# A hybrid diffusion step: the gate rows' chain in two parts by tokens, and the first output gate moved ahead of the gate transposes

## The chip, the cores and the metric

The kernel runs on one core of a Trainium2 chip. The metric is the device time of one execution in microseconds (us); lower is better. The engines are named as in the profile: PE is TensorE's matmul, PEld its weight load, DVE is VectorE, ACT is ScalarE, POOL is GpSimd, SP is SyncE. Each engine works through its own list of instructions; semaphores tie the lists together.

## The reference, cut to what matters

One layer takes 1024 sample (latent) tokens and 256 context tokens, 1280 in all, of width 1024. `u = RMSNorm(x)*(1+scale)+shift` goes through one wide projection. One of the three branches behind it is a bidirectional mLSTM with four heads. Its gates are 16 columns of the projection (input and forget gate, two directions, four heads). Per head and direction:

```
logf = log_sigmoid(f)
b    = cumsum(logf)                       # within a chunk
m_t  = max(b + m, max_s(b_t - b_s + i_s))   # running stabiliser
w_state = exp(bL - b + i - m_new);  decay = exp(bL + m - m_new)
h    = num / max(|den|, exp(-m_t))
y    = sigmoid(o_pre) * rmsnorm(h)
```

Sample tokens start both scans from a cached state (`m0`), context tokens from zero; no scan crosses from one kind of token to the other. `sigmoid(o_pre)` is the output gate, one projection of 128 columns a head.

## The kernel before, in words

Tokens lie in three groups (`GROUPS`): 512 and 512 sample tokens and 256 context tokens. Activations are held as pairs of fp32r tiles, a high and a low part (`uT[k][g]`, named `u0h`, `u0l`, and `u0c` for both parts of the context). A product (`dense`, lines 117 to 125) multiplies high by high, high by low and low by high, so a projection of 128 columns is 24 matmuls a group. Weights are loaded by SP, cut into `hi` on ACT and `lo` on DVE (`load_w`, lines 93 and 94).

Results go to PSUM banks. `ps_mm` is a ring of three banks for projections, `ps_sd` one of five for everything else. A fourth `ps_mm` product therefore waits until the first of the ring has been evicted, which ACT does (`evict_kqv`, line 329: `kT`, `vT`, `qT`, and `kq`, which holds k and q of the context).

In the first part of the program the engines' names stand for `Pinned` wrappers (line 43), which keep the instructions of an engine in the order in which they are written. Behind it a scheduler orders the rest, and may move what is not pinned into gaps.

The pinned loop `steps` goes over groups 1 and 2 and eight `k`. At each step it transposes a tile of x (`tr`), modulates one (`mc`: an ACT ACTIVATE into `val_u`, a DVE CAST and TENSOR_TENSOR into the pair `u..`), and adds one `k` to the first head's k and v (`p_k`, `p_v`). At step (2, 0) the gates of groups 0 and 1 are multiplied (`gates_of`, into `pg`); ACT copies them to `pgs`, and SP moves their low rows to other partitions (`pgl`). At step (2, 3) `gates_add` adds the halves on DVE into rows of `z`, 36 partitions by 1280 tokens. Behind the loop come the evictions of group 2, and the gates of group 2.

Then, unpinned, comes the chain of the gate rows: log-sigmoid (lines 419 to 428), the two kinds of scan (433 to 442), small copies of the values at chunk ends (`bL`, `mnew`, `mprev`), three exponentials (464, 468, 470), over all 1280 tokens at once. Lines 474 to 493 transpose the rows on PE (`pc`, 30 transposes) into `gcol` and spread the decays by one matmul (`pd`). The heads need `gcol` and `dmb`. While the chain runs, the scheduler fills PE with what needs only `uT`: q0 of groups 1 and 2, the first head's output gate (`p_o`), and k of the second head.

Of the kernel before, what the change touches and what calls it, by code (L numbers as in the profile page):

```python
# [7 lines left out]
F32 = mybir.dt.float32  # L8
F32R = mybir.dt.float32r
AF = mybir.ActivationFunctionType  # L10
ALU = mybir.AluOpType
# [18 lines left out]
I_XP, I_SU, I_Q, I_K, I_V, I_O, I_BR = 0, 4, 8, 12, 16, 20, 24  # L30
# [18 lines left out]
def hybrid_step(  # L49
# [7 lines left out]
    engines = nc.vector, nc.scalar, nc.gpsimd, nc.tensor  # L57
# [280 lines left out]
    nc.gpsimd.dma_start(sel, sel8)  # L338

    R36 = 36  # L340
    zr = [z[0:R36, i * T : (i + 1) * T] for i in range(7)]

    gparts = {}

# [15 lines left out]
    def gates_add(g):  # L360
        t0, n = GROUPS[g]
        both, low = (t[:, :n] for t in gparts[g])
        V.scalar_tensor_tensor(zr[0][:, t0 : t0 + n], both[0:36], bgt[:, 0:1], low[0:36], ALU.add, ALU.add)
        V.tensor_tensor(zr[1][:, t0 : t0 + n], both[64:100], low[64:100], ALU.add)


    begun = {nm: (w, []) for nm, w in (("k0", w_k0), ("v0", w_v0), ("q0", w_q0))}
# [44 lines left out]
    V, A, G, PE = engines  # L412
    gates_add(2)

    def chunks(ap):
        return ap.rearrange("p (c t) -> p c t", t=P)

    zi, zf, z2, z3, z4, z5, z6 = zr
    V.tensor_scalar(zf, zf, bgt[:, 1:2], None, ALU.add)
    A.activation(z2, zf, AF.Abs)  # L420
    A.activation(z6, z2, AF.Sigmoid)
    A.activation(z2, z2, AF.Exp, scale=-1.0)
    V.tensor_scalar(z3, z2, 1.0, None, ALU.add)
    A.activation(z4, z3, AF.Ln)
    V.scalar_tensor_tensor(z5, z3, -1.0, z2, ALU.add, ALU.subtract)
    V.tensor_tensor(z5, z5, z6, ALU.mult)
    V.tensor_tensor(z4, z4, z5, ALU.subtract)
    V.scalar_tensor_tensor(zf, zf, 0.0, z4, ALU.min, ALU.subtract)
    G.memset(z4, 1.0)
    G.memset(chunks(z4)[0:32, :, 0:1], 0.0)  # L430
    G.memset(chunks(z4)[32:36, :, 127:128], 0.0)
    rev = slice(None, None, -1)
    V.tensor_tensor_scan(z2[0:32], z4[0:32], zf[0:32], 0.0, ALU.mult, ALU.add)
    V.tensor_tensor_scan(z2[32:36, rev], z4[32:36, rev], zf[32:36, rev], 0.0, ALU.mult, ALU.add)
    for lo_, hi_, smp in ((0, NSAMP, True), (NSAMP, T, False)):
        ini = m0t if smp else None
        V.tensor_tensor_scan(
            z3[0:32, lo_:hi_], zf[0:32, lo_:hi_], zi[0:32, lo_:hi_],
            ini[0:32] if smp else 0.0, ALU.add, ALU.max)
        V.tensor_tensor_scan(  # L440
            z3[32:36, lo_:hi_][:, rev], zf[32:36, lo_:hi_][:, rev], zi[32:36, lo_:hi_][:, rev],
            ini[32:36] if smp else 0.0, ALU.add, ALU.max)
    bL = cp.tile([R36, NT], F32, name="bL")
    mnew = cp.tile([R36, NT], F32, name="mnew")
    mprev = cp.tile([R36, NT], F32, name="mprev")
    V.memset(mprev, 0.0)
    b3, m3 = chunks(z2), chunks(z3)
    V.tensor_copy(bL[0:32], b3[0:32, :, 127])
    V.tensor_copy(bL[32:36], b3[32:36, :, 0])
    V.tensor_copy(mnew[0:32], m3[0:32, :, 127])  # L450
    V.tensor_copy(mnew[32:36], m3[32:36, :, 0])
    V.tensor_copy(mprev[0:32, 0:1], m0t[0:32])
    V.tensor_copy(mprev[0:32, 1:8], mnew[0:32, 0:7])
    V.tensor_copy(mprev[0:32, 9:10], mnew[0:32, 8:9])
    V.tensor_copy(mprev[32:36, 7:8], m0t[32:36])
    V.tensor_copy(mprev[32:36, 0:7], mnew[32:36, 1:8])
    V.tensor_copy(mprev[32:36, 8:9], mnew[32:36, 9:10])
    G.dma_start(m_out[0], mnew[0:4, 9:10])
    G.dma_start(m_out[1], mnew[32:36, 8:9])
    bm = cp.tile([R36, NT], F32, name="bm")  # L460
    V.tensor_tensor(bm, bL, mnew, ALU.subtract)
    dec = cp.tile([R36, NT], F32, name="dec")
    V.tensor_tensor(dec, bm, mprev, ALU.add)
    A.activation(dec, dec, AF.Exp)

    V.tensor_tensor(zi, zi, z2, ALU.subtract)
    V.tensor_tensor(z2, z2, z3, ALU.subtract)
    A.activation(z5, z3, AF.Exp, scale=-1.0)
    V.tensor_tensor(chunks(z4), chunks(zi), bm.unsqueeze(2).to_broadcast([R36, NT, P]), ALU.add)
    A.activation(z4, z4, AF.Exp)  # L470


    gcol = cp.tile([P, 3, NT, 8], F32, name="gcol")
    for qi, src in enumerate((zi, z5, z4)):
        pc = ps_sd(f"pc{qi}")
        pcv = pc[:, 0 : NT * R36].rearrange("p (c j) -> p c j", j=R36)
        for c in range(NT):
            PE.transpose(pcv[:, c, :], src[:, c * P : (c + 1) * P], ident[0:R36, 0:R36])
        for d in range(2):
            V.tensor_copy(gcol[:, qi, :, 4 * d : 4 * d + 4], pcv[:, :, 32 * d : 32 * d + 4])  # L480
    GC, EM, EWS = (gcol[:, i] for i in range(3))

    dsel = tmp("dsel")[0:R36, 0:160].rearrange("p (q j c) -> p q j c", q=2, j=8)
    for qi, src in enumerate((dec, mprev)):
        V.tensor_tensor(
            dsel[:, qi], src.unsqueeze(1).to_broadcast([R36, 8, NT]),
            sel[0:36, :].unsqueeze(2).to_broadcast([R36, 8, NT]), ALU.mult)
    ones36 = tmp("ones36")[0:R36, 0:P]
    V.memset(ones36, 1.0)
    pd = ps_sd("pd")  # L490
    PE.matmul(pd[:, 0:160], ones36, dsel.rearrange("p q j c -> p (q j c)"), start=True, stop=True)
    dmb = cp.tile([P, 2, 8, NT], F32, name="dmb")
    V.tensor_copy(dmb.rearrange("p q j c -> p (q j c)"), pd[:, 0:160])
    decb, mpb = dmb[:, 0], dmb[:, 1]

    rhl = []
    for g in range(3):
# [38 lines left out]
    so = z[:, 7730:9010]  # L536
# [8 lines left out]

    def head_proj(h):
        tiles = {}
        kq = kq0 if h == 0 else slot(f"kq{h}", F32)
        for nm, idx in (("k", I_K), ("v", I_V), ("q", I_Q)):
            w, lst = begun.pop(f"{nm}{h}", (None, []))  # L550
            tiles[nm] = lst
            proj(idx + h, f"{nm}{h}", lambda g, ps: lst.append(evict_kqv(nm, h, g, ps, kq)), w=w, groups=range(len(lst), 3))
        return tiles["k"], tiles["v"], tiles["q"]

    def head(h, kT, vT, qT):
# [39 lines left out]
        def ev_o(g, ps):  # L595
            t0, n = GROUPS[g]
            A.activation(so[:, t0 : t0 + n], ps[:, :n], AF.Sigmoid)

        ssq = small([P, 16], f"ssq{h}")
        for g in range(3):  # L600
# [45 lines left out]
            if g == 0:  # L646
                proj(I_O + h, f"o{h}", ev_o)
            ps = ps_sd(f"th{h}_{g}")
            for cl in range(ncn):
# [886 lines left out]
```

## Time and profile before

| what | value |
|---|---|
| median of 3 runs | 1946.46 us (1945.74 to 1949.13) |
| profiled execution, its own time | 1947.31 us |
| its span, first to last instruction | 1945.5 us |
| mean granted TensorE clock | 0.994 |
| DMA | 313.32 MB, mean 161 GB/s |
| instructions on PE, DVE, ACT, POOL | 10136, 2207, 1768, 380 |

A row of the timeline gives the start, the duration, the engine, the line, the operation, and what is written from what; a bracket at its end gives the idle time of that engine just before and what ended it. L43 is the pinned helper, so pinned instructions all bear that line and are told apart by their tiles. A row of the waits gives the total, the number of times and the longest. PE's matmul ends are modelled.

### The profile page before, as it was taken

The page shows a single profiled execution, that of the slowest core. Times are in us where ns is not written, and L with a number is a line of the kernel's source. Part 1 is how long each engine was busy: PE and PEld are TensorE (multiplying, and loading weights), DVE is VectorE, ACT ScalarE, POOL GpSimd, SP SyncE. Part 2 cuts the span into 40 slices and gives each one's busy share as a digit, 9 for nine tenths or more (in the row PEclk, how much of TensorE's full clock was granted, in tenths as well). Part 3 has the DMA queues.
Part 4 walks back from the last instruction along what each step waited for, and adds up shares of the span by engine and source line. Part 5 has one row for each costly group of instructions (what it writes and reads, how often), then busy time and mean ns, then how long its engine had stood idle before and what let it go on. Part 6 is the DMA issues. An engine that isn't in the chain of part 4 may idle for free.

```text
span 1945.5 us, 28129 instructions
## 1 busy us (share of the span) xinstructions
PE 1903.0 (98%) x10136; PEld 1627.5 (84%) x10136; DVE 1294.0 (67%) x2207; ACT 861.7 (44%) x1768; POOL 378.2 (19%) x380
## 2 busy tenths in 40 slices
PE   6999999999999999999999999999999999999998
PEld 3778888998788888888888887888888888888886
DVE  6574443347759889875675599888776655744665
ACT  7444464653243333343123374555454545443443
POOL 1200001107302424220000015444431110000003
PEclk9999999999999999999999999999999999999999
DMA  9211111012635445469522435776773586654444
GB/s 361 85 59 33 43 39 40 27 56 70 203 119 165 149 158 164 153 211 321 163 97 98 152 120 212 253 264 246 259 269 136 193 333 203 210 170 151 165 133 159
DMA packets 149318, 313.32 MB, mean 161 GB/s; under 512 B 17550, under 2 KB 40818, under 8 KB 147130
## 3 DMA queue, kind: packets, MB, share of 16 engines
q1 hardware_dynamic: 107354, 220.73, 33.9%
q0 software_dynamic: 15520, 57.75, 7.8%
q10 hardware_dynamic: 26304, 33.04, 4.7%
q8 instruction: 79, 1.29, 0.3%
q14 instruction: 61, 0.50, 0.1%
HBM read 217.59 MB, written 93.36 MB: 160 GB/s over the span
## 4 chain that ended last, share of the span: by engine, by line
PE 87%; DVE 4%; DMA 3%; POOL 2%; ACT 1%; issue 1%; SPq 0%; POOLq 0%; ACTq 0%; DVEq 0%
PE w L1403 6%; PE w L1404 6%; PE w L1405 6%; PE pb L1050 3%; PE pb L1051 3%; PE pb L1052 3%; PE fT L892 3%; PE fT L890 3%; PE fT L891 3%; PE fB L891 2%; PE fB L890 2%; PE fB L892 2%; PE fT_g L892 2%; PE fT_g L890 2%; PE fT_g L891 2%; PE po L1168 2%
## 5 line engine op out<-in xcount | busy, mean ns | idle before, releaser
L1242 POOL TENSOR_TENSOR z<-z 128x512 f32<-128x512 f32 x64 | 100.1, 1564 | 123.3 <-DMA z<-in_w_ff 120.6
L947 DVE TENSOR_TENSOR z<-z 128x512 f32<-128x512 f32 x112 | 88.7, 792 | 2.5
L527 POOL PARTITION_ALL_REDUCE acc<-acc x16 | 54.6, 3446 | 184.0 <-DVE acc L521 113.6
L521 DVE SCALAR_TENSOR_TENSOR acc<-z,scond,acc 128x512 f32<-128x512 f32 x112 | 86.1, 816 | 0.0
L1357 POOL TENSOR_TENSOR rs_y<-rs_y,neghalf 128x1 f32<-128x1 f32 x10 | 9.6, 966 | 333.0 <-DVE rs_y L1356 333.0
L1208 ACT ACTIVATE z<-z 128x512 f32<-128x512 f32 x64 | 40.5, 632 | 69.8 <-DVE z L956 36.7
L972 ACT ACTIVATE z<-z 128x512 f32<-128x512 f32 x48 | 30.3, 632 | 59.1 <-DVE z L956 23.1
L130 POOL TENSOR_TENSOR rs_h<-rs_h,neghalf 128x4 f32<-128x4 f32 (+1 forms) x12 | 10.9, 910 | 200.5 <-DVE rs_h L129 200.3
L653 DVE SCALAR_TENSOR_TENSOR yc<-th,ccol,z 128x512 f32<-128x512 f32 (+1 forms) x12 | 7.9, 661 | 58.2 <-PE th L651 58.2
L1056 DVE TENSOR_TENSOR sg<-pb,sg 128x512 f32<-128x512 f32 (+1 forms) x48 | 28.7, 600 | 26.7 <-PE pb L1052 26.5
L881 ACT CAST hi_wb<-raw_wb 128x512 fp32r<-128x512 f32 x24 | 14.8, 620 | 64.4 <-PE pb L1051 37.6
L1209 ACT ACTIVATE z<-z 128x512 f32<-128x512 f32 x64 | 40.3, 629 | 1.1
L1171 DVE TENSOR_TENSOR po<-po,gt 128x512 f32<-128x512 f32 (+1 forms) x24 | 14.6, 607 | 35.1 <-PE po L1170 35.0
L1233 POOL DMA_DIRECT2D scr_s<-x x48 | 26.3, 549 | 53.1 <-DVE x L1227 47.6
L738 POOL TENSOR_TENSOR z<-z 128x1024 f32<-128x1024 f32 (+13 forms) x20 | 33.6, 1702 | 6.9 <-ACT z L722 4.6
L528 POOL TENSOR_TENSOR acc<-acc,bt 1x512 f32<-1x512 f32 x16 | 23.5, 1480 | 58.4 <-issue 58.4
L1174 ACT ACTIVATE po<-z 128x512 f32<-128x512 f32 (+1 forms) x24 | 12.7, 529 | 48.5 <-DVE z L1173 34.2
L587 DVE SCALAR_TENSOR_TENSOR z<-z,dmb,kv 128x129 f32<-128x129 f32 x56 | 16.6, 345 | 21.8 <-PE kv L576 21.3
L1057 DVE TENSOR_TENSOR z<-z,sg 128x512 f32<-128x512 f32 (+1 forms) x48 | 28.7, 601 | 1.2
L640 DVE TENSOR_TENSOR den<-den,gcol 128x2 f32<-128x2 f32 x40 | 6.2, 159 | 31.0 <-ACT den L639 29.9
L43 PE MATMUL pm<-wah,shl 128*4 128x512 f32 x32 | 13.8, 461 | 13.2 <-ACT wah L43 13.2
L130 POOL TENSOR_TENSOR rs_f<-rs_f,neghalf 128x4 f32<-128x4 f32 (+1 forms) x3 | 3.3, 1092 | 116.9 <-DVE rs_f L129 116.9
(5136 smaller groups left out, 7288.9 us busy)
## 6 DMA issues: line engine op xcount, KB each, us to landing
z<-in_w_ff SPq DMA_DIRECT2D x64, 512.0 KB, 5.5
z<-in_w_ada SPq DMA_DIRECT2D x64, 256.0 KB, 3.1
scr_t<-z POOLq DMA_DIRECT2D x16, 1024.0 KB, 4.9
z<-in_w_in SPq DMA_DIRECT2D x24, 512.0 KB, 4.3
scr_g<-z ACTq DMA_DIRECT2D x48, 256.0 KB, 2.0
sg<-scr_g SPq DMA_DIRECT2D x48, 256.0 KB, 4.5
scr_h<-z ACTq DMA_DIRECT2D x48, 256.0 KB, 3.6
scr_s<-x POOLq DMA_DIRECT2D x48, 256.0 KB, 4.3
```

The lines of the kernel that those rows point to most:

```text
L521: V.scalar_tensor_tensor(acc[j], raw, scond[:, k, j : j + 1], acc[j], ALU.mult, ALU.add)
L890: PE.matmul(ps, whi[:, s], ahi, start=first and k == ks[0], stop=False)
L891: PE.matmul(ps, whi[:, s], alo, start=False, stop=False)
L892: PE.matmul(ps, wlo[:, s], ahi, start=False, stop=end and k == ks[-1])
L947: V.tensor_tensor(out, x, y, op)
L1050: PE.matmul(pb[:, :n], whi[:, s], yh, start=kc == 0, stop=False)
L1051: PE.matmul(pb[:, :n], whi[:, s], yl, start=False, stop=False)
L1052: PE.matmul(pb[:, :n], wlo[:, s], yh, start=False, stop=kc == 3)
L1242: G.tensor_tensor(out, x, y, ALU.subtract)
L1403: PE.matmul(banks[j], h_[:, s], rh, start=fp == 0, stop=False)
L1404: PE.matmul(banks[j], l_[:, s], rh, start=False, stop=False)
L1405: PE.matmul(banks[j], h_[:, s], rl, start=False, stop=fp == NFP - 1)
```

## The change

The chain becomes a function `gate_rows(groups)`, called twice: for groups 0 and 1 (1024 sample tokens) inside the pinned loop at step (2, 6), and for group 2 (256 context tokens) behind the pinned part. The transposes become `gate_columns(groups)`, called twice as well. q0 of groups 1 and 2, the first head's output gate and k of the second head are now written out around them. DVE, ACT and POOL are unpinned behind the loop as before, while PE stays pinned until the second `gate_columns`. The gates are added at (2, 6) instead of (2, 3). The multiplication by a sigmoid in the correction of the logarithm is left out, with its row of `z`; the free room lets `so`, the output gate, lie beside the gate rows.

```diff
-        if (g, k) == (2, 3):
-            gates_add(0)
-            gates_add(1)
+        if (g, k) == (2, 6):
+            gate_rows((0, 1))
...
     gates_of(2)
-    V, A, G, PE = engines
-    gates_add(2)
+    V, A, G = engines[:3]
+
+    for g in (1, 2):
+        ps = ps_mm(f"p_q0{g}")
+        dense(ps, w_q0, uT, g)
+        begun["q0"][1].append(evict_kqv("q", 0, g, ps, kq0))
+    so = z[:, 7730:9010]
...
+    w_o0 = load_w(w_in[I_O], "o0")
+    for g in range(3):
+        ps = ps_mm(f"p_o0{g}")
+        dense(ps, w_o0, uT, g)
+        ev_o(g, ps)
+    gate_rows((2,))
+    gate_columns((0, 1))
+    kq1 = slot("kq1", F32)
+    w_k1 = load_w(w_in[I_K + 1], "k1")
+    begun["k1"] = w_k1, []
+    for g in range(3):
+        ps = ps_mm(f"p_k1{g}")
+        dense(ps, w_k1, uT, g)
+        begun["k1"][1].append(evict_kqv("k", 1, g, ps, kq1))
+    gate_columns((2,))
+    PE = engines[3]
```

The new functions, cut to their core (`y..` are the rows' columns from `lo_` to `hi_`):

```diff
+    def gate_rows(groups):
...
+        G.memset(y4, 1.0)
...
+        for g in groups:
+            gates_add(g)
+        V.tensor_scalar(yf, yf, bgt[:, 1:2], None, ALU.add)
+        A.activation(y2, yf, AF.Abs)
+        A.activation(y2, y2, AF.Exp, scale=-1.0)
+        V.tensor_scalar(y3, y2, 1.0, None, ALU.add)
+        V.scalar_tensor_tensor(y5, y3, -1.0, y2, ALU.add, ALU.subtract)
+        A.activation(y3, y3, AF.Ln)
+        V.tensor_tensor(y3, y3, y5, ALU.subtract)
+        V.scalar_tensor_tensor(yf, yf, 0.0, y3, ALU.min, ALU.subtract)
...
+        A.activation(dec[:, cc], dec[:, cc], AF.Exp)
+        A.activation(y5, y3, AF.Exp, scale=-1.0)
+        V.tensor_tensor(yi, yi, y2, ALU.subtract)
+        V.tensor_tensor(y2, y2, y3, ALU.subtract)
+        V.tensor_tensor(chunks(y4), chunks(yi), bm[:, cc].unsqueeze(2).to_broadcast([R36, nch, P]), ALU.add)
+        A.activation(y4, y4, AF.Exp)
+
+    def gate_columns(groups):
...
+        for qi, src in enumerate((yi, y5, y4)):
...
+            for c in range(nch):
+                PE.transpose(pcv[:, c, :], src[:, c * P : (c + 1) * P], ident[0:R36, 0:R36])
...
+        PE.matmul(pd[:, 0 : 16 * nch], ones36, dsel.rearrange("p q j c -> p (q j c)"), start=True, stop=True)
```

The four scans (the running maximum, then the cumulative sum, each for 32 and for 4 partitions) stand where the third mark is.

The first place is DVE's list at the end of the loop. Before, the four gate adds (`z<-pgs`) stand in front of the last three pairs `u5c` to `u7c`, and behind these come the low parts of the weights of o and k:

```order
L43 SCALAR_TENSOR_TENSOR z<-pgs_920,bgt,pgl_921 36x512
L43 TENSOR_TENSOR z<-pgs_920,pgl_921 36x512
L43 SCALAR_TENSOR_TENSOR z<-pgs_941,bgt,pgl_942 36x512
L43 TENSOR_TENSOR z<-pgs_941,pgl_942 36x512
L43 CAST u5c<-val_u_5_1000 128x256
L43 TENSOR_TENSOR u5c<-val_u_5_1000,u5c 128x256
```

On the same engine of the changed kernel the adds stand behind `u7c`, and the sample rows follow at once (`36x1024`), with the two low parts between them:

```order
L43 CAST u7c<-val_u_7_1026 128x256
L43 TENSOR_TENSOR u7c<-val_u_7_1026,u7c 128x256
L43 SCALAR_TENSOR_TENSOR z<-pgs_928,bgt,pgl_929 36x512
L43 TENSOR_TENSOR z<-pgs_928,pgl_929 36x512
L43 SCALAR_TENSOR_TENSOR z<-pgs_949,bgt,pgl_950 36x512
L43 TENSOR_TENSOR z<-pgs_949,pgl_950 36x512
L94 TENSOR_TENSOR lo_o_1164<-raw_o_1161,hi_o_1163 128x1024
L43 TENSOR_SCALAR z<-z,bgt 36x1024
L94 TENSOR_TENSOR lo_k_1323<-raw_k_1320,hi_k_1322 128x1024
L43 TENSOR_SCALAR z<-z 36x1024
```

So the pairs moved ahead of the adds, and the sample rows' chain moved ahead of everything that DVE does for the context's gates.

The second place is ACT's list behind the last modulation. Before, it cuts the weights and evicts k and v of group 2, the context's gates and q0, and then begins the rows (`z<-z`):

```order
L93 CAST hi_o_1420<-raw_o_1418 128x1024
L43 ACTIVATE kq_669<-p_k_957 128x256
L93 CAST hi_k_1673<-raw_k_1671 128x1024
L43 ACTIVATE vT_2_1046<-p_v_958 128x256
L43 COPY pgs_1065<-pg_1048 128x256
L329 ACTIVATE qT_1_1204<-p_q_1179 128x512
L329 ACTIVATE kq_669<-p_q_1206 128x256
L93 CAST hi_v_1759<-raw_v_1757 128x1024
L420 ACTIVATE z<-z 36x1280
```

In the changed kernel, in ACT's list from the second weight on:

```order
L93 CAST hi_k_1322<-raw_k_1320 128x1024
L43 ACTIVATE z<-z 36x1024
L43 ACT_TABLE_LOAD
L43 ACTIVATE z<-z 36x1024
L43 ACT_TABLE_LOAD
L43 ACTIVATE z<-z 36x1024
L43 ACT_TABLE_LOAD
L43 ACTIVATE dec<-dec 36x8
L43 ACTIVATE z<-z 36x1024 x2
L43 ACTIVATE kq_669<-p_k_965 128x256
L43 ACTIVATE vT_2_1085<-p_v_966 128x256
L43 COPY pgs_1104<-pg_1087 128x256
```

All the sample rows' ACT work now stands ahead of the three evictions.

The third place is PE's list where q0 of group 2 begins (`p_q<-u0c`). Before, the context's gates stand ahead of it, and q0 of group 1 lies further ahead, between the steps of k and v:

```order
L43 MATMUL pg_1048<-u5c,wgs_804 128x256 x2
L43 MATMUL pg_1048<-u6c,wgs_804 128x256 x2
L43 MATMUL pg_1048<-u7c,wgs_804 128x256 x2
L123 MATMUL p_q_1206<-u0c,hi_q_665 128x256
L124 MATMUL p_q_1206<-u0c,hi_q_665 128x256
L125 MATMUL p_q_1206<-u0c,lo_q_666 128x256
```

In the changed kernel PE's list has q0 of group 1 directly ahead of it:

```order
L43 MATMUL p_q_1108<-u7h_873,hi_q_665 128x512
L43 MATMUL p_q_1108<-u7l_874,hi_q_665 128x512
L43 MATMUL p_q_1108<-u7h_873,lo_q_666 128x512
L43 MATMUL p_q_1135<-u0c,hi_q_665 128x256 x2
L43 MATMUL p_q_1135<-u0c,lo_q_666 128x256
```

q0 of group 1 moved behind the context's gates; o0, the sample transposes, k of the second head and the context's transposes follow in the order of the diff.

More of the change, by code (lines that the diff above doesn't have):

```diff
@@ L340, in hybrid_step @@
     R36 = 36
-    zr = [z[0:R36, i * T : (i + 1) * T] for i in range(7)]
+    zr = [z[0:R36, i * T : (i + 1) * T] for i in range(6)]
     gparts = {}
@@ L364, in gates_add, with chunks @@
         V.tensor_tensor(zr[1][:, t0 : t0 + n], both[64:100], low[64:100], ALU.add)
+    def chunks(ap):
+        return ap.rearrange("p (c t) -> p c t", t=P)
+    zi, zf, z2, z3, z4, z5 = zr
+    rev = slice(None, None, -1)
+    bL = cp.tile([R36, NT], F32, name="bL")
+    mnew = cp.tile([R36, NT], F32, name="mnew")
+    mprev = cp.tile([R36, NT], F32, name="mprev")
+    bm = cp.tile([R36, NT], F32, name="bm")
+    dec = cp.tile([R36, NT], F32, name="dec")
+    gcol = cp.tile([P, 3, NT, 8], F32, name="gcol")
@@ new lines, in hybrid_step @@
+    GC, EM, EWS = (gcol[:, i] for i in range(3))
+    dmb = cp.tile([P, 2, 8, NT], F32, name="dmb")
+    decb, mpb = dmb[:, 0], dmb[:, 1]
+    V.memset(mprev, 0.0)
+    def gate_rows(groups):
+        lo_, hi_ = GROUPS[groups[0]][0], sum(GROUPS[groups[-1]])
+        smp = lo_ == 0
+        c0, c1 = lo_ // P, hi_ // P
+        nch = c1 - c0
+        yi, yf, y2, y3, y4, y5 = (t[:, lo_:hi_] for t in zr)
+        cc = slice(c0, c1)
+        G.memset(y4, 1.0)
+        G.memset(chunks(y4)[0:32, :, 0:1], 0.0)
+        G.memset(chunks(y4)[32:36, :, 127:128], 0.0)
+        for g in groups:
[8 more added lines that the diff above has]
+        V.scalar_tensor_tensor(yf, yf, 0.0, y3, ALU.min, ALU.subtract)
+        for r, d in ((slice(0, 32), slice(None)), (slice(32, 36), rev)):
+            V.tensor_tensor_scan(
+                y3[r][:, d], yf[r][:, d], yi[r][:, d], m0t[r] if smp else 0.0, ALU.add, ALU.max)
+        for r, d in ((slice(0, 32), slice(None)), (slice(32, 36), rev)):
+            V.tensor_tensor_scan(y2[r][:, d], y4[r][:, d], yf[r][:, d], 0.0, ALU.mult, ALU.add)
+        b3, m3 = chunks(y2), chunks(y3)
+        V.tensor_copy(bL[0:32, cc], b3[0:32, :, 127])
+        V.tensor_copy(bL[32:36, cc], b3[32:36, :, 0])
+        V.tensor_copy(mnew[0:32, cc], m3[0:32, :, 127])
+        V.tensor_copy(mnew[32:36, cc], m3[32:36, :, 0])
+        if smp:
+            V.tensor_copy(mprev[0:32, 0:1], m0t[0:32])
+            V.tensor_copy(mprev[32:36, 7:8], m0t[32:36])
+        V.tensor_copy(mprev[0:32, c0 + 1 : c1], mnew[0:32, c0 : c1 - 1])
+        V.tensor_copy(mprev[32:36, c0 : c1 - 1], mnew[32:36, c0 + 1 : c1])
+        if not smp:
+            G.dma_start(m_out[0], mnew[0:4, 9:10])
+            G.dma_start(m_out[1], mnew[32:36, 8:9])
+        V.tensor_tensor(bm[:, cc], bL[:, cc], mnew[:, cc], ALU.subtract)
+        V.tensor_tensor(dec[:, cc], bm[:, cc], mprev[:, cc], ALU.add)
+        A.activation(dec[:, cc], dec[:, cc], AF.Exp)
[4 more added lines that the diff above has]
+        A.activation(y4, y4, AF.Exp)
@@ L411, in hybrid_step @@
     gates_of(2)
-    V, A, G, PE = engines
-    gates_add(2)
[L415 to L491, printed above, removed]
```

33 lines of the change are left out of this document (24 added, 9 removed).

## The prediction

> **What bounds the kernel now.** I read the page's busy shares first, then the chain that ended last, then who TensorE waited for.
>
> ```profile
> PE 1903.0 (98%) x10136; PEld 1627.5 (84%) x10136; DVE 1294.0 (67%) x2207; ACT 861.7 (44%) x1768; POOL 378.2 (19%) x380
> PE 87%; DVE 4%; DMA 3%; POOL 2%; ACT 1%; issue 1%; SPq 0%; POOLq 0%; ACTq 0%; DVEq 0%
> PE pm L43 <- ACT wah L43: 13.2, 2, 11.9
> PE pc L478 <- DVE z L466: 3.6, 1, 3.6
> PE p_k L123 <- ACT z L597: 0.3, 1, 0.3
> ```
>
> TensorE (PE) is busy 98% of the span and carries 87% of the chain, so time is won or lost only where PE stands still or runs at a lower clock. The longest waits are at the start (pm), which the change leaves alone. The second place is the gate transposes, `pc`, which wait 3.6 us for VectorE's gate rows. Only this place can be improved. The timeline of PE around it, then the granted clock (the figure behind the five busy times of each stretch):
>
> ```profile
> 117.82 0.50 PE L123 MATMUL p_k<-u0h,hi_k 128*128 128x512 f32 x1 [0.33 <-ACT z L597]
> 134.29 1.97 PE L478 MATMUL pc<-cst,z 36*128 36x36 f32 x20 [3.62 <-DVE z L466]
> 138.50 0.63 PE L123 MATMUL p_v<-u0h,hi_v 128*128 128x512 f32 x1
> 134.00:135.00 1.00, 0.71 (x10) 0.74 (x11) 0.95 (x7) 0.00 (x0) 0.00 (x0) 0.89 0.01 0
> 141.00:142.00 1.00, 1.00 (x4) 0.77 (x3) 1.00 (x1) 0.00 (x0) 0.00 (x0) 0.70 0.00 0
> 142.00:143.00 1.00, 1.00 (x6) 0.83 (x5) 0.17 (x1) 0.00 (x0) 0.00 (x0) 1.00 0.00 0
> ```
>
> The stall has a second price. Behind it the granted clock is half: from 134.8 (0.89 in the first microsecond means 0.22 us of it at half) to 141.4 (0.70 means 0.6 us at half), so 6.6 us at half speed, 3.3 us lost; a matmul of 512 columns shows 0.63 there. If the change removed the stall with everything behind it, the gain would be 3.6 + 3.3 + 0.3 = 7.2 us, 0.37% of the run. More cannot be had there.
>
> **What the change puts in ScalarE's queue.** The sample rows' chain is now written at step (2, 6) of the loop, in the part that keeps program order. On ScalarE (ACT) its Abs, Exp, Ln and three further Exps stand, by the order shown above, ahead of the eviction of `p_k` of group 2, of `p_v` of group 2, of the context gates and of q0's group 1. Before, the first two came right behind their matmuls:
>
> ```profile
> 98.47 1.05 ACT L93 CAST hi_o<-raw_o 128x1024 fp32r<-128x1024 f32 x1 [8.00 <-PE p_k L43]
> 99.43 0.38 ACT L43 ACTIVATE kq<-p_k 128x256 f32<-128x256 f32 x1
> 100.67 0.28 PE L123 MATMUL p_q<-u0c,hi_q 128*128 128x256 f32 x1
> ```
>
> PE's q0 of group 2 (`p_q<-u0c`) takes its bank from `ps_mm`, a ring of three. The three before it are p_k of group 2, p_v of group 2 and q0 of group 1, so it needs p_k's bank, which `kq<-p_k` frees. Before, that was at 99.43 + 0.38 = 99.8, and q0 began at 100.67 without waiting. Now the eviction waits for the last sample Exp, and that for VectorE (DVE). Whether a blocked ACTIVATE really holds those behind it shows in this trace already:
>
> ```profile
> 123.17 0.39 PE L125 MATMUL p_k<-u7h,lo_k 128*128 128x512 f32 x1
> 125.07 1.27 ACT L468 ACTIVATE z<-z 36x1280 f32<-36x1280 f32 x1 [4.29 <-DVE z L440]
> 126.25 0.58 ACT L329 ACTIVATE kT<-p_k 128x512 f32<-128x512 f32 x1
> ```
>
> p_k was complete at 123.6, but its eviction ran at 126.25, behind an Exp that waited for a scan. There it cost nothing, since its bank was next wanted by p_v at 138.50.
>
> **When PE arrives.** Up to q0's group 2, PE has the same matmuls before and after; only q0's group 1 (24 matmuls) moves from between the k0/v0 steps to behind the context gates. So it arrives at 100.7 again, if the k0/v0 steps don't run dry without that filler.
>
> ```profile
> 89.58 0.47 PE L123 MATMUL p_q<-u0h,hi_q 128*128 128x512 f32 x1
> 97.32 0.40 PE L43 MATMUL p_k<-u6c,hi_k 128*128 128x256 f32 x2
> 98.03 0.40 PE L43 MATMUL p_k<-u7c,hi_k 128*128 128x256 f32 x2
> 89.91 0.57 ACT L43 ACTIVATE val_u<-pt_u,sh,a 128x256 f32<-128x256 f32 x1 [0.37 <-PE pt_u L43]
> ```
>
> A step of six matmuls takes 0.71 us (97.32 to 98.03). Without q0 the steps u3c to u7c follow from 89.6 on, and u7c is wanted at 92.4. Its source val_u is there at 90.5, and DVE has it at 91.5 (next paragraph). So PE is not held up.
>
> **When the chain ends.** DVE's rows of before:
>
> ```profile
> 89.37 0.73 DVE L43 SCALAR_TENSOR_TENSOR z<-pgs,bgt,pgl 36x512 f32<-36x512 f32 x1
> 91.61 0.69 DVE L43 TENSOR_TENSOR z<-pgs,pgl 36x512 f32<-36x512 f32 x1
> 92.33 0.29 DVE L43 CAST u5c<-val_u 128x256 fp32r<-128x256 f32 x1
> 93.99 0.42 DVE L43 TENSOR_TENSOR u7c<-val_u,u7c 128x256 fp32r<-128x256 f32 x1
> 99.56 1.23 DVE L94 TENSOR_TENSOR lo_o<-raw_o,hi_o 128x1024 fp32r<-128x1024 f32 x1 [5.14 <-ACT hi_o L93]
> 105.83 0.88 DVE L419 TENSOR_SCALAR z<-z,bgt 36x1280 f32<-36x1280 f32 x1
> 106.74 1.28 ACT L420 ACTIVATE z<-z 36x1280 f32<-36x1280 f32 x1 [1.23 <-DVE z L419]
> 108.05 1.27 ACT L421 ACTIVATE z<-z 36x1280 f32<-36x1280 f32 x1
> 109.34 1.28 ACT L422 ACT_TABLE_LOAD   x1
> 110.64 1.27 ACT L422 ACTIVATE z<-z 36x1280 f32<-36x1280 f32 x1
> 111.94 0.82 DVE L423 TENSOR_SCALAR z<-z 36x1280 f32<-36x1280 f32 x1 [4.10 <-ACT z L422]
> 112.80 1.48 DVE L425 SCALAR_TENSOR_TENSOR z<-z 36x1280 f32<-36x1280 f32 x1
> 118.94 2.34 DVE L437 TENSOR_TENSOR_SCAN z<-z,m0t 32x1024 f32<-32x1024 f32 x1
> 131.89 0.16 DVE L450 COPY mnew<-z 32x10 f32<-32x10 f32 x1
> 136.26 1.47 DVE L469 TENSOR_TENSOR z<-z,bm 36x1280 f32<-36x1280 f32 x1
> ```
>
> No row of width 1024 but the scans is in this trace. A 36x512 TENSOR_TENSOR takes 0.69, a 36x1280 row 1.47 to 1.48; on the line between them 1024 columns take 1.22, which I use as 1.25 from start to start (the trace leaves some 0.03 between such rows). For ACT, 1.28 at 1280 columns and 0.58 for a 512-column eviction (the kT row above) give 1.05; for TENSOR_SCALAR four fifths of 0.88 and 0.82, 0.70 and 0.66. The bounds are the rows at both ends: six DVE rows, two TENSOR_SCALARs and four ACT rows at the full 1280 times add 2.8 us (6 x 0.26 + 0.34 + 4 x 0.23); six DVE and four ACT rows at the 512 times take off 5.0 (6 x 0.53 + 4 x 0.47). I take the line between, since the columns lie nearer to 1280.
>
> - The pairs u5c to u7c took 92.33 to 94.41, behind the four gate adds. Now they stand ahead, from 89.37: done at 91.5. The adds' 2.93 us (89.37 to 92.30) follow: 94.4.
> - lo_o 1.2 (its hi_o needs p_k's last matmul, now at 93.0, so it is there by 94.1), bias 0.7: 96.3.
> - Abs 1.05, a table load 1.28, Exp 1.05, with hand-overs: 99.8. The old sigmoid (L421) is gone.
> - Plus one 0.66, the STT 1.25: 101.75. Ln 1.05 (its table load is hidden behind these two): 102.9. Two more rows of 1.25: 105.4.
> - Four scans of 2.35 start to start: 114.8. Eight copies, bm, dsel and dec of 0.1 to 0.2 each, 1.5 together: 116.3.
> - yi, y2 and y4 rows of 1.25 with dsel and a memset between them (0.4): 120.4. ACT's last Exp 1.05: 121.5. kq<-p_k 0.38: 121.9. PE goes on at 122.0.
>
> So PE stands still from 100.7 to 122.0: **21.3 us**. The cover that the chain had before, q0's second group, all of o0 and most of k1, now stands behind the wait.
>
> **What else moves.** The 24 sample transposes then find all rows ready, so the old 3.62 us stall goes; the 0.33 us at 117.82 goes too, since o0 is evicted with more room. The context's chain is four times shorter; its start is the copy of its gates and the transfer of their low rows:
>
> ```profile
> 100.91 0.38 ACT L43 COPY pgs<-pg 128x256 f32<-128x256 f32 x1
> 104.89 0.48 DVE L363 SCALAR_TENSOR_TENSOR z<-pgs,bgt,pgl 36x256 f32<-36x256 f32 x1 [1.26 <-DMA pgl<-pgs]
> ```
>
> That was 3.6 us from the copy's end (101.3) to DVE's start. Now the copy ends at 122.7, behind the evictions of p_k and p_v, and DVE starts at 126.3. By the same steps at 256 columns (some 0.45 a row, 0.4 an ACTIVATE, 0.7 a scan, lo_v's 1.23 between them) dec is ready at 137.5, and o0's first eviction, behind it and a table load, ends at 139.4. PE needs that bank for k1 at about 142 or 143 (122.0, and 16.8 for q0 and o0, which before ran from 100.7 to 117.5, and 3.3 for the clock). So nothing waits there, with about 3 us to spare, and the last six transposes come at about 158, long after their rows. Transposes are as many as before (30), the added `pd` matmul, six small gcol copies and two memsets fall on engines with room. The added table loads (1.28 each, ACT busy 44%) lie in that room. SP's loads come behind freed weight slots, well ahead of use; the y4 memsets move up in POOL's queue, ahead of some stores of u, and the two m_out stores come earlier there; POOL is busy 19%. So these count as zero; if the 3 us margin fails, the next stall is priced below.
>
> PE resumes at half clock. I take the same 6.6 us as behind the old stall, so that term cancels. A stall near 29 us in this run shows 6.4 us of the same:
>
> ```profile
> 28.00:30.00 2.00, 0.93 (x6) 0.37 (x5) 1.26 (x4) 1.13 (x2) 0.05 (x1) 0.74 1.05 406
> 34.00:36.00 2.00, 2.00 (x9) 1.65 (x8) 1.97 (x5) 0.76 (x2) 0.54 (x1) 0.55 1.03 422
> ```
>
> The Trainium skill (TensorE: Matmul & The Clock Gate, Part 1, "What's actually happening") gives full speed back after one busy window of about 3.4 us. Here the trace has about two such windows in both places, and differs. By the page the loss would be an estimated 1.7 instead of 3.3 us and the sum 1.6 us smaller.
>
> The skill also prices a table switch (ScalarE: Activation LUTs, "What ACT_TABLE_LOAD costs") at the 1283 ns load and a drain of about 1380 ns. The trace has the load but no drain: L421 ends at 109.32, the load runs 109.34 to 110.62, the Exp starts at 110.64. By the page the one load on the path alone would lengthen the stall by an estimated 1.4 us; I go by the rows.
>
> **Sum:** +21.3 − 3.6 − 0.3 + 0 = **+17.4 us**. The profiled execution took 1947.3, 0.85 above the median of 1946.46; on it this gives 1964.7, on the median's scale **1963.9**.
>
> **Rivals.**
> 1. *A second stop.* The context's chain comes more than 3 us later than I worked out (its low rows' transfer behind raw_v and raw_q, which SP issues ahead of it), and k1's first group waits for o0's eviction behind the context's Exp. Against it: raw_v and raw_q wait only for lo_o and lo_k, done near 97. Price up to 5 us: 1969. Chance 0.12.
> 2. *Not slower: the bank is free in time.* If p_k's bank came free by 100.7, as it did, PE would run on through o0 to 117.5, as before. It would then find yi just ready (117.6) but y4 only at 121.5, and stand for 3 to 4 us, the old price again: 1946 to 1947. What decides is one eviction, ahead of or behind the sample Exps on ACT. The order speaks against it, and that the change does not do what the order says is the only way to it. Chance 0.05.
> 3. *Faster: the whole stall goes.* This needs rival 2 and the chain 4 us shorter as well: 1946.5 − 7.2 = 1939.3. Chance 0.02.
>
> **How the numbers follow.** My case has 0.81, and its own range runs from 1959 (5.0 less, the 512 rows) to 1967 (2.8 more, the 1280 rows). The half-clock stretch lies between nothing and the rows' full length, as PE's restart may fall late in it; half of it, 1.6 us less, takes the low end to 1957. The second stop takes the high end to 1969. That leaves out the two rivals with shorter times, 0.07, and a little of the rest. About 0.2% (3.9 us) is what a measurement of this kernel can tell from no change; faster 0.02, same 0.05, slower 0.93.
>
> **What would show it.** Right: PE idle some 21 us ahead of q0's group 2, released by ACT's kq; ACT's kq<-p_k near 122, directly behind a 36x1024 Exp; the idle time before the gate transposes gone; half clock for some 6 us after the stall. Wrong: p_q<-u0c starting near 101; DVE's last sample row ending well before 120; or a second wait of PE in k1.

## The result

| | before | after |
|---|---|---|
| median of 5 runs, us | 1949.13 (1945.74 to 1955.21) | 1963.39 (1962.11 to 1964.22) |
| ratio of the two | | 1.0073, 95% interval 1.0060 to 1.0086 |
| profiled execution, us | 1947.31 | 1963.39 |
| its span, us | 1945.5 | 1961.6 |

The kernel became 0.73% slower, at a time 0.5 us from the forecast. The busy times on the page of the changed kernel:

```profile
PE 1902.9 (97%) x10138; PEld 1628.7 (83%) x10138; DVE 1296.3 (66%) x2232; ACT 867.8 (44%) x1778; POOL 383.2 (20%) x383
```

From its list of waits the largest row, which is new (us in total, times, longest):

```profile
PE p_q L43 <- ACT kq L43: 20.7, 1, 20.7
```

PE has as much busy time as before (1902.9 against 1903.0); the time went into one new wait, and the wait for the gate transposes is gone from the list. ACT's timeline at that place (start, duration, and in brackets the idle time before with what ended it):

```profile
96.44 1.28 ACT L43 ACT_TABLE_LOAD   x1
97.73 1.06 ACT L43 ACTIVATE z<-z 36x1024 f32<-36x1024 f32 x1
100.80 1.06 ACT L43 ACTIVATE z<-z 36x1024 f32<-36x1024 f32 x1 [0.70 <-DVE z L43]
101.87 1.28 ACT L43 ACT_TABLE_LOAD   x1
115.58 0.21 ACT L43 ACTIVATE dec<-dec 36x8 f32<-36x8 f32 x1 [12.42 <-DVE dec L43]
119.25 1.06 ACT L43 ACTIVATE z<-z 36x1024 f32<-36x1024 f32 x1 [2.52 <-DVE z L43]
120.22 0.36 ACT L43 ACTIVATE kq<-p_k 128x256 f32<-128x256 f32 x1
```

PE's timeline there:

```profile
120.63 0.79 PE L43 MATMUL p_q<-u0c,hi_q 128*128 128x256 f32 x2 [20.71 <-ACT kq L43]
125.92 0.63 PE L43 MATMUL p_o<-u0h,hi_o 128*128 128x512 f32 x1
140.05 1.67 PE L43 MATMUL pc<-cst,z 36*128 36x36 f32 x24
```

And DVE's, the four scans of the sample rows and the row that the last Exp waits for:

```profile
104.39 4.69 DVE L43 TENSOR_TENSOR_SCAN z<-z,m0t 32x1024 f32<-32x1024 f32 x2
109.11 4.59 DVE L43 TENSOR_TENSOR_SCAN z<-z 32x1024 f32<-32x1024 f32 x2
117.96 1.20 DVE L43 TENSOR_TENSOR z<-z,bm 36x1024 f32<-36x1024 f32 x1
```

ACT is idle for 12.42 us ahead of dec's Exp, with `kq<-p_k` ready and queued behind it: p_k's last matmul had ended before 93 us. PE stands from 99.92 (120.63 less 20.71) until that eviction ends. The sample transposes (`pc`, x24) then follow o0 without idle time. The clock behind the stall, by one-microsecond windows: the granted clock, the third figure from the end, is 0.50 up to 126 us, and then

```profile
126.00:127.00 1.00, 1.00 (x5) 0.82 (x5) 0.59 (x2) 1.00 (x1) 0.00 (x0) 0.77 0.00 0
```

0.77 means 0.46 us at half, so PE, back at work, ran at half clock from 120.63 to 126.46: 5.8 us, 2.9 lost.

### The profile page after: what moved, and what is told of

Same layout as the page of the kernel before. It is cut to its first block, busy times and chain, and to the rows that moved or that the text cites. A ratio compares the mean times of both kernels' runs of the same rounds, so it can differ in the third digit from the quotient of the medians.

```text
span 1961.6 us, 28173 instructions
## 1 busy us (share of the span) xinstructions
PE 1902.9 (97%) x10138; PEld 1628.7 (83%) x10138; DVE 1296.3 (66%) x2232; ACT 867.8 (44%) x1778; POOL 383.2 (20%) x383
## 4 chain that ended last, share of the span: by engine, by line
PE 51%; DVE 4%; DMA 1%; issue 1%; ACT 1%; POOL 0%; ACTq 0%; POOLq 0%; DVEq 0%; SPq 0%
PE w L1433 6%; PE w L1435 6%; PE w L1434 6%; PE fT L922 3%; PE pb L1081 3%; PE pb L1080 3%; PE fT L920 3%; PE pb L1082 3%; PE fT L921 3%; PE fB L920 2%; PE fB L921 2%; PE fB L922 2%; PE po L1200 2%; PE po L1199 2%; PE po L1198 2%; PE fc L920 2%
## 5 line engine op out<-in xcount | busy, mean ns | idle before, releaser
L130 POOL TENSOR_TENSOR rs_h<-rs_h,neghalf 128x4 f32<-128x4 f32 (+1 forms) x12 | 10.9, 910 | 215.2 <-DVE rs_h L129 215.0
L621 DVE SCALAR_TENSOR_TENSOR z<-z,dmb,kv 128x129 f32<-128x129 f32 x56 | 16.8, 345 | 21.6 <-PE kv L610 21.2
```

## The experiments

The theory: one eviction, `kq<-p_k`, stands in ACT's in-order queue behind Exps that wait for DVE's chain, and PE wants the bank that it frees. The rivals: the long chain holds PE wherever the eviction stands; transfers do; or the moved output gate has a part in it. The times of before, run beside each group, had medians of 1949.0 to 1950.5, so each kernel is judged by its ratio.

**The chain made longer.** DVE does the two running-maximum scans of the sample rows twice (the second pass gives the same values).

```diff
-        for r, d in ((slice(0, 32), slice(None)), (slice(32, 36), rev)):
+        for r, d in ((slice(0, 32), slice(None)), (slice(32, 36), rev)) * (2 if smp else 1):
             V.tensor_tensor_scan(y3[r][:, d], ...
```

> The changed kernel with the two running-maximum scans of the sample rows done twice; the second pass gives the same values. It adds two scans of 2.35 us, 4.7 us, to the chain on DVE. Theory (the chain's length sets the end of the stall): the wait at q0's group 2 grows from 20.7 to 25.4 us, and the time by the same 4.7 us to 1968.1. Rival (a transfer or another queue sets it, and the chain has slack): the wait stays at 20.7 us and the time at 1963.4.

Its list of PE's waits:

```profile
PE p_q L43 <- ACT kq L43: 25.5, 1, 25.5
```

Measured: 25.5 us and 1968.61 us (ratio 1.0099, 1.0084 to 1.0114). 4.8 us of scan became 4.8 us of stall and 5.2 us of time: the chain has no slack, and transfers are out as what ends the stall.

**The evictions moved ahead of the chain.**

```diff
         if (g, k) == (2, 6):
-            gate_rows((0, 1))
...
     gates_of(2)
+    gate_rows((0, 1))
     V, A, G = engines[:3]
```

> The call for the sample rows moves from step (2, 6) of the loop to right behind the context gates, so ACT evicts p_k and p_v of group 2 and copies the gates ahead of the chain's first Abs. Theory (the stall before q0's group 2 is the eviction that stands behind the chain's Exps): no wait of PE over 1 us at q0's group 2 (20.7 us with the change). The chain itself ends later, near 125 to 130 us, while PE reaches the gate transposes near 117, so two waits appear there, some 9 us for the first rows and some 3 us for the last Exp's; 12 us in all, and the time is near 1955 us. Rival (the long chain on DVE and ACT as such holds PE, wherever it stands in ACT's queue, or the transfers do): about 20 us of wait remain at q0's group 2, and 1963 us.

Its waits of PE:

```profile
PE pc L43 <- DVE dec L424: 7.6, 1, 7.6
PE pc L43 <- ACT z L43: 3.9, 1, 3.9
```

Measured: no wait at q0; 7.6 and 3.9 us at the transposes; 1954.46 us (1.0027, 1.0016 to 1.0039). The stall moved to the chain's own consumer, where it is 9 us shorter, since o0 now covers part of it. The first row names the context's `dec`, which ran from 123.96 to 124.10; what these transposes take is the sample's row that DVE ended at 124.04, beside it. The context's scans (116.36 to 119.17) had slipped in ahead of that row on DVE.

**Only ACT's queue changed.** The rows stay at step (2, 6) up to `dec`; the last three Exps and the rows between are written behind the evictions.

```diff
         if (g, k) == (2, 6):
-            gate_rows((0, 1))
+            gate_rows((0, 1), last=False)
...
     gates_of(2)
+    gate_rows((0, 1), first=False)
     V, A, G = engines[:3]
```

> The changed kernel with the sample rows cut in two: everything up to Ln, the scans and dec stays at step (2, 6); the last three Exps and the rows between them are written behind the evictions of p_k and p_v of group 2 and the gates' copy. DVE's chain stays where it was, only ACT's queue changes. Theory (the evictions wait behind an Exp that waits for DVE): kq<-p_k now runs behind Ln, near 102 us instead of 120.22, so the wait at q0's group 2 shrinks from 20.7 to 2 or 3 us; PE then comes to the transposes near 119 us and waits there for the last Exp (3 to 7 us, since context rows may slip in between). 1949 to 1954 us. Rival (DVE's long chain holds PE): 20 us remain at q0's group 2.

The eviction and PE behind it, from the timelines of ACT and of PE:

```profile
101.81 0.36 ACT L43 ACTIVATE kq<-p_k 128x256 f32<-128x256 f32 x1
102.23 0.65 PE L43 MATMUL p_q<-u0c,hi_q 128*128 128x256 f32 x2 [2.25 <-ACT kq L43]
```

Its waits of PE at the transposes:

```profile
PE pc L43 <- ACT z L43: 4.1, 2, 3.3
PE pc L43 <- DVE z L43: 2.0, 1, 2.0
```

Measured: the eviction runs at 101.81, right behind Ln, and the stall shrinks from 20.7 to 2.3 us with DVE's chain in its place; 1953.42 us (1.0020, 1.0010 to 1.0030). What is left of the loss are the waits at the transposes: the context's rows slipped into ACT's queue ahead of the sample's Exps, three rows of 36x256, an eviction and their table loads from 115.93 to 123.02, with dec's Exp behind them.

**A bank instead of the eviction.** The eviction stays behind the chain, but q0's group 2 and o0 take banks of the ring of five.

```diff
     for g in (1, 2):
-        ps = ps_mm(f"p_q0{g}")
+        ps = (ps_mm if g == 1 else ps_sd)(f"p_q0{g}")
...
-        ps = ps_mm(f"p_o0{g}")
+        ps = ps_sd(f"p_o0{g}")
```

> The changed kernel with the sample rows where the change put them, but q0's group 2 and the three groups of the first output gate take their PSUM banks from the ring of five that stands free at that time (the number of banks is unchanged). Theory (PE waits for a bank, not for the chain): no wait at q0's group 2; PE runs on through o0 to about 116.4 us (99.8, 2.9 for q0's group 2, 13.7 for o0) and stands there for the sample rows' last Exp near 121 to 123 us, 5 to 6 us in one or two pieces, with some 3 us of half clock behind; the time is 1946 to 1949 us, no different from before. Rival (the chain as such holds PE): the wait of 20.7 us stays, 1963 us.

The only row over 1.1 us in its list of PE's waits from 60 to 200 us:

```profile
PE pc L43 <- ACT z L43: 4.9, 2, 3.7
```

Measured: no wait at q0, 4.9 us at the transposes, and 1952.56 us (1.0014, 1.0005 to 1.0023). So it is the bank that PE waits for, not the chain. That the time is a little over before's, not equal, comes late: the first `fB_g` matmul starts at 561.9 here and at 561.8 before, but from the first `po` to the first `w` matmul it takes 532.4 us against 528.4 (and 526.3 in the changed kernel); why, no run tells.

**A fourth bank for the groups,** taken from the ring of five.

```diff
-        return pp.tile([P, 512], F32, tag="mm", name=name, bufs=3)
+        return pp.tile([P, 512], F32, tag="mm", name=name, bufs=4)
...
-        return pp.tile([P, 512], F32, tag="sd", name=name, bufs=5)
+        return pp.tile([P, 512], F32, tag="sd", name=name, bufs=4)
```

> The changed kernel with four PSUM banks for the matmul groups and four instead of five for the states and other small products; no instruction moves by hand. Theory (PE waits only for p_k's bank): q0's group 2 takes the fourth bank and starts near 100 us without a wait. The next groups then find banks late: p_k's and p_v's evictions at 121 still come behind the last sample Exp, so o0's first groups wait instead, since four banks hold only q0 group 2 more: some 0 to 7 us of waits if the freed banks suffice, at the worst 18 us at o0's first group. Likeliest 1947 to 1950 us, with an unknown cost of the fewer small banks in the heads, 0 to 5 us. Rival (something else than the bank holds q0): the 20.7 us wait stays at q0's group 2, and 1963 us or more.

Its waits of PE at o0, and two that are new in the stages behind the heads:

```profile
PE mx L841 <- ACT ya L795: 4.0, 1, 4.0
PE p_o L43 <- ACT z L512: 3.5, 2, 2.8
PE p_o L43 <- ACT kq L329: 2.3, 1, 2.3
PE pp L793 <- ACT ya L795: 2.1, 1, 2.1
```

The first `fB_g` matmul, behind the heads, in PE's timeline of this kernel (the changed one has it at 577.25, shown further down):

```profile
576.09 0.40 PE L920 MATMUL fB_g<-u0h,a_g0h 128*128 128x512 f32 x1
```

Measured: the 20.7 us are gone and 5.8 us of waits stand at o0, so 14.9 us are saved there. At the first `fB_g` only 1.2 of them are left (577.25 less 576.09), and by its end this kernel is 3.0 us behind the changed one (spans 1964.6 and 1961.6): 1965.39 us (1.0082, 1.0065 to 1.0099). The theory's part was right, but not the price of a bank taken from the small products, expected at 0 to 5 us: it is some 18 us (14.9 and 3.0), most of it ahead of `fB_g`. How much of it is the missing bank itself, and how much the order that PE's matmuls then take, this run does not separate.

**The output gate back in the head.**

```diff
-    w_o0 = load_w(w_in[I_O], "o0")
-    for g in range(3):
-        ps = ps_mm(f"p_o0{g}")
-        dense(ps, w_o0, uT, g)
-        ev_o(g, ps)
...
-            if g == 0 and h > 0:
+            if g == 0:
```

> The changed kernel with the first head's output gate written in the head again, as before the change; the sample rows stay at step (2, 6). Theory (the stall belongs to the rows' place alone): the wait at q0's group 2 stays at 20.7 us (20 to 21.5), and the time is 1963 us within 2 us. The gate transposes then follow q0 directly and their rows are all there, so no new wait appears. Rival (the moved output gate carries part of the loss): 1955 us or less.

The stall's row in its list of waits:

```profile
PE p_q L43 <- ACT kq L43: 20.7, 1, 20.7
```

The head's first transposes and the first `fB_g` in PE's timeline, in this kernel:

```profile
141.32 0.66 PE L590 MATMUL tk<-cst,kT 128*128 128x128 f32 x4
570.75 0.40 PE L915 MATMUL fB_g<-u0h,a_g0h 128*128 128x512 f32 x1
```

and in the changed one:

```profile
156.63 0.66 PE L595 MATMUL tk<-cst,kT 128*128 128x128 f32 x4
577.25 0.40 PE L920 MATMUL fB_g<-u0h,a_g0h 128*128 128x512 f32 x1
```

Measured: the stall is the same to the tenth, but the time is 1956.70 us (1.0040, 1.0025 to 1.0055), 6.7 below the changed kernel. I had expected no difference. From the first transposes to `fB_g` this kernel takes 429.4 us and has all of o0 in it; an equal projection of 72 matmuls takes 13.78 us (the row is shown below), so the rest takes 415.6, against 420.6 in the changed kernel: 5.0 us saved where the heads and the stages behind them run. Another 1.0 comes from the half clock, 3.8 us instead of 5.8 (the last section has the rows), and 0.6 from an earlier start (q0's group 2 at 120.03, not 120.63). Of the 5.0, 3.4 are waits: between these two places the changed kernel has four (1.4, 1.2, 0.9 and 0.7 us), this one a single one of 0.8. So the stall is the rows' alone, and moving o0's 72 matmuls out of the head has a price of its own. That this price is not o0's in particular, the third filled kernel below shows.

**The stall filled.** Three kernels put more matmuls ahead of all transposes. The first keeps the chain where the change put it and the other ring's banks of the run above; k of the second head and the first group of its v are the cover.

```diff
-    gate_columns((0, 1))
...
-        ps = ps_mm(f"p_k1{g}")
+        ps = (ps_mm if g else ps_sd)(f"p_k1{g}")
...
+    w_v1 = load_w(w_in[I_V + 1], "v1")
+    ps = ps_mm("p_v10")
+    dense(ps, w_v1, uT, 0)
...
+    gate_columns((0, 1))
     gate_columns((2,))
```

> As the kernel with o0 in the other ring's banks, and k of the second head (its first group in the same ring) and the first group of the second head's v written ahead of all gate transposes. Theory: nothing is left that PE waits for between 90 and 150 us, save perhaps 2 us for the context's last rows, whose chain starts behind the sample's and ends near 138 us, while PE reaches the transposes at about 135. Against the changed kernel that is 20.7 us and 3.0 us of half clock less: 1939.7 us, with the 2 us and their half clock at the worst 1944. Rival (moving more fillers ahead starves the heads, as the run with o0 in the head suggests in the other direction): 3 to 5 us more than that, 1943 to 1945, with no wait before 150 us.

Measured: waits of 0.9 us at k1 and twice 1.8 us in the heads, none at the transposes; 1946.37 us (0.9980, 0.9970 to 0.9989). It lies nearer to the rival (1943 to 1945) than to the theory (1939.7).

The second has the same cover, but the evictions ahead of the chain and the context's rows in program order:

```diff
-        if (g, k) == (2, 6):
-            gate_rows((0, 1))
...
     gates_of(2)
+    gate_rows((0, 1))
...
-    gate_rows((2,))
+    V, A = (Pinned(tc, e) for e in engines[:2])
+    gate_rows((2,))
+    V, A = engines[:2]
```

> The sample rows behind the evictions of group 2 and the gates' copy (as in the run with 7.6 and 3.9 us of waits at the transposes), the context's rows in program order right behind, and k of the second head and the first group of its v written ahead of all gate transposes. Theory: PE reaches the transposes at about 135 us, when all rows (sample near 127, context near 133) are there; no wait over 1 us between 90 and 150; 1939.7 us (1963.4 less 20.7 and 3.0), 7 us below before. Rival (the heads lack the fillers that moved ahead): no wait there, but 3 to 5 us are given back between 150 and 600 us, 1943 to 1945.

From its list of PE's waits:

```profile
PE p_k L123 <- ACT z L511: 3.5, 2, 1.8
```

The first of the two in PE's timeline:

```profile
189.84 0.50 PE L123 MATMUL p_k<-u0h,hi_k 128*128 128x512 f32 x1 [1.76 <-ACT z L511]
```

And ACT's timeline ahead of it:

```profile
187.26 1.28 ACT L511 ACT_TABLE_LOAD   x1
189.19 0.60 ACT L511 ACTIVATE z<-p_o 128x512 f32<-128x512 f32 x1 [0.65 <-DVE yc L689]
```

Measured: no wait over 0.3 us from 90 to 150, but two in the heads, 3.5 us together: the next head's output gate comes so early that its eviction, behind a table load, still waits for `yc` to have read the old gate, and holds a bank meanwhile. 1944.61 us (0.9973, 0.9963 to 0.9982). The rival was right about how much is given back.

The third has the evictions ahead of the chain, k and all of v of the second head as cover, and o0 in the head again:

```diff
-    w_o0 = load_w(w_in[I_O], "o0")
...
+    for g in range(3):
+        ps = ps_mm(f"p_v1{g}")
+        dense(ps, w_v1, uT, g)
```

> As the kernel before in this list, but the cover ahead of the gate transposes is k and all of v of the second head (27.4 us), and the first output gate is written in the head again. Theory: PE reaches the transposes at about 130 us; the sample rows are there or 1 us late, the context's rows up to 3 us late; as many matmuls have moved ahead as in the changed kernel, so the heads run as there: 1940 to 1945 us. Rival (the output gate in the head is worth the 6.7 us that its move back gave, whatever else moved): 1933 to 1937.

The last sample Exp in ACT's timeline and the sample transposes in PE's:

```profile
121.15 1.06 ACT L43 ACTIVATE z<-z 36x1024 f32<-36x1024 f32 x1 [2.04 <-DVE z L43]
130.07 1.67 PE L43 MATMUL pc<-cst,z 36*128 36x36 f32 x24
```

Two pieces of its chain that ended last (start, length, what), the cover:

```profile
102.58 13.78 PE p_k L43 x72
116.36 13.78 PE p_v L43 x72
```

Measured: 1940.74 us, ratio 0.9958 (0.9944 to 0.9972), so 8.2 us below before by the ratio; it beats both kernels. PE runs from 94 to 139 us without a wait, and the rows are there 8 us before it comes for them. The prediction's bound for a stall that goes with all that hangs on it, 7.2 us, is what came, within the interval (5.5 to 10.9).

The rival (o0 in the head is worth some 6.7 us whatever else moves, 1933 to 1937) did not come. Where q0's group 2 and `fB_g` begin in this kernel:

```profile
99.55 0.40 PE L43 MATMUL p_q<-u0c,hi_q 128*128 128x256 f32 x2
553.89 0.40 PE L922 MATMUL fB_g<-u0h,a_g0h 128*128 128x512 f32 x1
```

That is 454.3 us. The changed kernel takes 456.6 (120.63 to 577.25), of which 2.9 are lost to the half clock, so 453.7; o0 in the head 450.7 (120.03 to 570.75), less 1.9, so 448.8. So v of the second head ahead of the transposes costs the heads as much as o0 did, some 5 us, and four waits of 4.2 us in all are there again (1.3, 1.1, 1.1 and 0.7). In these kernels it is not o0 that counts, but that 72 matmuls fewer are left for the heads. Before has four waits of 4.2 us there as well; its free order ran o0 ahead too.

**Less cover.** As the third, but only v's first group ahead of the sample columns, and PE's order free from there on.

```diff
-    for g in range(3):
+    for g in range(1):
         ps = ps_mm(f"p_v1{g}")
...
     gate_columns((0, 1))
-    gate_columns((2,))
-    PE = engines[3]
+    PE = engines[3]
+    gate_columns((2,))
```

> As the kernel with k1 and v1 ahead, but only the first group of v1 stands ahead of the sample columns, and PE's order is free from there on. Theory: PE reaches the sample columns near 122 us, when their last Exp (ended at 122.2 there) is just there: a wait below 1.5 us; the rest of v1 is left as a filler, and by what the output gate in the head was worth (13.7 us of filler for some 5 us) the 8.2 us give up to 3 us: 1938 to 1941 us. Rival (the heads begin when the context's columns are there, so the filler only changes places): the same as with all of v1 ahead, 1940.7 within 1 us, or worse by a wait at the columns with its half clock, 1944.

Its waits of PE at the context's transposes:

```profile
PE pc L442 <- DVE z L43: 2.8, 1, 2.8
PE pc L442 <- ACT z L43: 1.6, 1, 1.6
```

The two windows in which the clock changes:

```profile
135.00:136.00 1.00, 0.06 (x1) 0.06 (x1) 0.97 (x6) 0.41 (x2) 0.00 (x0) 0.73 0.00 0
145.00:146.00 1.00, 1.00 (x8) 1.00 (x7) 0.04 (x1) 0.59 (x1) 0.00 (x0) 0.65 0.00 0
```

Measured: the sample columns came without a wait, but the context's come too early by 2.8 and 1.6 us, and the clock is at half from 135.46 to 145.70. 1948.49 us (0.9989, 0.9981 to 0.9998), above what either expectation gave: of the gain a thousandth is left.

## Why the prediction was right

- **ACT's queue** (the eviction behind the last sample Exp): shown by the row at 120.22, by the split rows (20.7 to 2.3 us) and by the doubled scan (25.5 us).
- **The bank** of the ring of three: shown by the two kernels that gave PE another.
- **When PE arrives**: forecast 100.7, measured 99.92; the k0/v0 steps did not run dry, and the whole stretch came 0.9 us earlier.
- **When the chain ends**: forecast 121.9, measured 120.58 (120.22 and 0.36). About 0.9 of the 1.3 us is the earlier start; the steps fit (1024 columns on DVE 1.20, forecast 1.22; on ACT 1.06, forecast 1.05; four scans, 104.39 to 113.70, 9.3, forecast 9.4). The stall is 20.7 instead of 21.3.
- **The half clock**: taken as unchanged at 6.6 us, measured 5.8. The prediction misread the rows that it shows: 0.70 means 0.60 us at half, so the stretch of before ends at 141.60 and is 6.8 us long (3.4 lost), and so is the one near 29 us (28.96 to 35.80, taken as 6.4). The loss is 0.5 us less. The Trainium skill's single window of about 3.4 us (TensorE: Matmul & The Clock Gate, Part 1), counted from PE's restart, would make it an estimated 1.7 us lost. The trace shows 2.9: the window is 3.41 us long here too, but it does not begin with the restart (last section).
- **Table loads**: the Exp at 97.73 starts 0.01 us after its load ends (96.44 and 1.28), and the load 0.02 us after the Abs ahead of it (95.36 and 1.06). The drain of some 1380 ns that the Trainium skill adds (ScalarE: Activation LUTs, "What ACT_TABLE_LOAD costs") is not in this trace either.
- **The second stop** did not come. Its margin was forecast at 3 us; o0's first eviction ended at 136.77 (136.17 and 0.60) and PE wanted the bank at 141.95, so it was 5.2.

  The two rows, from the timelines of ACT and PE of the changed kernel:

```profile
136.17 0.60 ACT L512 ACTIVATE z<-p_o 128x512 f32<-128x512 f32 x1
141.95 0.50 PE L43 MATMUL p_k<-u0h,hi_k 128*128 128x512 f32 x1
```

- **The sum**: +17.4 forecast; by the measured terms 20.7 − 3.6 − 0.3 − 0.5 = +16.3, and the spans differ by 16.1. That the time is only 0.5 us off is luck: the profiled execution of before stood 0.85 us above the median shown then, and the forecast took that off, while that of the changed kernel is its median itself (1947.3 + 16.1 = 1963.4). With five runs before's median is 1949.13, and the medians are 14.3 us apart (by the interval 11.7 to 16.8): the mechanism and the terms were right, and the sum, just outside that interval, was a little large.
- **The term that was zero by luck of the order**: o0's move. Against before it costs nothing, since there the free order of PE had o0 ahead of the transposes too (its first matmul at 103.56); but against leaving it in the head with nothing moved in its place it costs some 5 us, which the prediction had not seen.

Of the rival "not slower: the bank is free in time", the other-banks kernel is the case itself: the waits at the transposes came nearly as it said (3 to 4 us, measured 4.9), and the time lies 0.14% above before's, where it had put them equal.

## What to carry over

Before a long chain that crosses engines is moved forward in a program, read what stands behind its waiting instructions on each in-order engine: an eviction of 0.36 us behind an Exp that waits for scans held TensorE for 20.7 us, and an order in which the evictions stand ahead (or the next group has another bank) is worth more than the chain's own earlier start. Then count the cover: the chain's end less TensorE's arrival must be filled with matmuls whose buffers are free. That cover has a price later: 72 matmuls more ahead, the output gate's or those of the next head's v alike, cost the heads about 5 us here, so take no more than the chain needs.

## What was not expected of the hardware

How long the clock stays at half behind a wait hardly depends on the wait: 3.4 us behind 2.25 us (the split rows), 6.8 behind 3.6 (before), 5.8 behind 20.7 (after), 3.8 behind the same 20.7 with o0 in the head, 3.0 behind 25.5 (doubled scan). In these stretches the smallest wait behind which the clock fell is 1.96 us (the split rows, at 122.90); one of 1.76 us (the second filled kernel, at 188 us) left it at full. Two waits close together, 2.8 and 1.6 us, cost 10.2 us at half clock, the second falling inside the stretch of the first. The windows of the split rows:

```profile
102.00:103.00 1.00, 0.77 (x4) 0.77 (x5) 1.00 (x1) 1.00 (x4) 0.00 (x0) 0.71 0.00 0
105.00:106.00 1.00, 1.00 (x8) 1.00 (x7) 0.73 (x2) 0.00 (x0) 0.00 (x0) 0.58 0.00 0
122.00:123.00 1.00, 0.41 (x6) 0.44 (x7) 0.78 (x2) 1.00 (x1) 0.00 (x0) 0.95 0.00 0
```

of the second filled kernel:

```profile
189.00:190.00 1.00, 0.16 (x1) 0.16 (x2) 1.00 (x5) 0.79 (x2) 0.00 (x0) 1.00 0.64 33
```

of o0 in the head:

```profile
123.00:124.00 1.00, 1.00 (x7) 1.00 (x7) 0.90 (x2) 0.00 (x0) 0.00 (x0) 0.60 0.00 0
```

and of the doubled scan:

```profile
128.00:129.00 1.00, 1.00 (x8) 1.00 (x7) 0.17 (x1) 0.00 (x0) 0.00 (x0) 0.63 0.17 56
```

PE went on at 120.03 and 125.79 in the last two.

What sets the length shows when the stretches are counted from the fall of the clock, the standstill included. The windows of the fall in the changed kernel, with o0 in the head and with the doubled scan:

```profile
102.00:103.00 1.00, 0.00 (x0) 0.00 (x0) 1.00 (x1) 1.00 (x1) 0.00 (x0) 0.78 0.00 0
103.00:104.00 1.00, 0.00 (x0) 0.00 (x0) 0.96 (x2) 0.00 (x0) 0.00 (x0) 0.66 0.00 0
104.00:105.00 1.00, 0.00 (x0) 0.00 (x0) 0.96 (x2) 0.00 (x0) 0.00 (x0) 0.92 0.00 0
```

So the clock was at half from 102.56 to 126.46 (23.90 us), from 103.32 to 123.80 (20.48) and from 104.84 to 128.74 (23.90); in the split rows from 102.42 to 105.84 (3.42) and from 122.90 to 133.14 (10.24), with less cover for 10.24, and before for 6.82. These are 7, 6, 7, 1, 3, 3 and 2 times 3.41 us. In these runs the clock changes only at the ends of windows of some 3.41 us, which do not begin with PE's restart. What a wait costs behind its end therefore depends on where in such a window PE goes on: in the changed kernel 1.0 us into one (119.63), and the clock came back only at the end of the next; in the doubled scan 0.5 us into one (125.32), and it came back at the end of that one. Why before needed two windows, though PE worked from 134.29 on, these runs do not tell.
